# One encoder block on one core: keys and values of the first group computed token by token, V scaled by a column of 1/rms read back through DRAM

## The chip, the cores and the metric

The kernel runs on one NeuronCore of a Trainium2 chip. The metric is the device time of the core in microseconds; the median of the runs counts. One further execution was profiled, and all rows of the trace are from it.

## The reference

One block of an encoder for 256 tokens of width 2048, in float32. Shortened:

```python
u = rmsnorm(h, norm_mix_g)                       # D_MODEL 2048, SEQ 256
z = u @ w_in
b_a, c_a, v_a, q, k, v, gl_a, gl_b = split(z)    # 3 x 1024, q 1024, k 256, v 256, 2 x 2048
y_a = (b_a * centred_dwconv3(c_a * v_a, conv_a_w)) @ w_out_a
q, k = rope(q), rope(k)                          # 16 query heads, 4 key heads, 64 wide
att = banded_window_attention(q, k, v, sink)     # |distance| <= 128, a sink per head
y_b = att @ w_o_attn
h = h + (sigmoid(gl_a + b_a') * y_a + sigmoid(gl_b + b_b') * y_b) @ w_mix_out
up = centred_dwconv3(rmsnorm(h, norm_ffn_g) @ ffn_w_up, ffn_conv_w) + ffn_conv_b
h = h + (silu(up[:D_FF]) * up[D_FF:]) @ ffn_w_down
return rmsnorm(h, norm_final_g)
```

## The kernel before, in words

**Arithmetic.** Every float32 product is three products in TensorE's fp32r format. Weights and activations are split into a high part (a rounded copy) and a low part (what the rounding left), and hi x hi, hi x lo and lo x hi are added in one PSUM bank. ACT makes a weight chunk's high part (L203, tile `whi`), the DVE its low part (L214, tile `wlo`). The input x, transposed, stands in `xs` as 16 k-tiles of 128 rows with 256 columns hi and 256 columns lo; it is multiplied by the norm's weights there, while the division by the rms comes after the products.

**Two ways of a product.** A *single block* takes 128 output features: the weights are stationary, x is moving. L261 is a matmul of `whi` with 512 columns (x hi and lo), L262 one of `wlo` with 256 columns (x hi). The result has features on partitions and tokens along the row, as rotary embedding and scores need it. A *quad* takes 512 features at once: x is stationary, 128 tokens at a time, and the weights are moving, 512 columns. For each of the two halves of the tokens there are three matmuls, L237 (x hi, `whi`), L238 (x lo, `whi`) and L239 (x hi, `wlo`). Its result has tokens on partitions. To be turned, it goes through 32x32 transposes on the DVE (L330), a write to a DRAM tile `way` (L314) and four reads that put the blocks where they belong (L318, and L322 for a copy with the two halves of every head exchanged, which rotary embedding wants).

**The order of the work** is written out by hand. `run` goes through a list of chunks. Chunks 0 to 15 are the first group, one k-tile each: six single blocks K0, K1, V0, V1, Q0, Q1. Chunks 16 to 19 are the other two early query blocks (`w_q`, Q2 and Q3, eight k-tiles a chunk). Then come chunks of two k-tiles of a quad: 20 to 75 for seven quads of `w_in`, the first of them the last four query tiles (`rope_four`), the others the conv mixer; from 76 on the gates, then the output projections, the mixing matrix and the feed-forward part; at the end some single blocks again and the final norm. For each chunk c, `run` first issues the fetch of chunk c+6 (SyncE, L188), the cast of chunk c+3 (ACT) and the subtraction of chunk c+2 (DVE), and then chunk c's matmuls. `raw` has five buffers, `whi` four, `wlo` three, so these instructions wait for buffers that older chunks free.

Everything else is hung between chunks. A counter `now` goes up by one after each chunk's matmuls. An epilogue is a Python generator, and each `yield 1` in it means "go on after the next chunk". So "step n" below is what is issued after n chunks of matmuls, ahead of the fetch, cast and subtraction of that turn. All engines take their instructions in this written order, each in its own queue, and the waits for data are added by the framework. A tile with one buffer can be given out anew while its old contents have readers still to come in the written order: the first write of the new contents then waits for the last of them.

**What stands around the change.** `r1` (due at step 14) sums the squares of x, multiplies by a matrix of ones on TensorE (L390, step 16), and at step 18 has 1/rms in `r`, the same on all partitions, along the tokens; cos and sin are multiplied by it (L499). Singles are evacuated by `total` (L291 on ACT, L295 on the DVE), which adds the two halves of a bank. Keys and early queries then run through `rope`: four transfers on SyncE exchange the halves of a head (L535, tile `rot`), the DVE multiplies by cos and sin and adds (L537, L541, L542), `twice` copies the two heads of a tile to both halves of the partitions by four transfers (L550, tile `two`, one buffer), and ACT and the DVE make high and low parts: `kh` and `kl` for K (L557, L559), `qs` for queries (L566, L570). V is multiplied by `r`, turned on TensorE by four 128x128 transposes with an identity from the constants (`epi_v`, L619), and copied to `vtok` (L621), tokens on partitions.

`TURNS` (L127) has some single blocks issue lo before hi, at positions 1, 5, 9 and 15 from where `turns` was called: in the first group from chunk 4, and in the single blocks at the kernel's end.

Attention runs in ten blocks at steps 29 + 21t // 4. A block t issues the scores of two heads (L631, L632, eight matmuls), whose softmax runs on DVE and ACT and whose probabilities go through DRAM as above; from t = 3 on every second block also multiplies the probabilities by `vtok` (L684).

Of the kernel before, what the change touches and what calls it, by code (L numbers as in the profile page):

```python
# [45 lines left out]
C_ID = C_MASK + T  # L46
C_END = C_ID + P

# [5 lines left out]
def hybrid_block_kernel(  # L54
# [81 lines left out]
    taken = [0]  # L136

    def quad_banks():
# [3 lines left out]
        if q < IN_QUADS:  # L142

            where = l2 if q % 2 else [(lin, "ps"), (aps, "tp2")]
        else:
            where = ([(aps, "s0"), (aps, "s1")], [(aps, "tp2"), (aps, "av")], l2)[(q - IN_QUADS) % 3]
        return [pool.tile([P, QUAD * P], F32, tag=tag, name="pq") for pool, tag in where]

    def run(groups):
# [21 lines left out]

        def size(c):

            w, blocks, _ = chunks[c]
            return len(blocks) if w is None else w.shape[1]
# [41 lines left out]
        for c, (_, blocks, _) in enumerate(chunks):  # L217
# [7 lines left out]
            for i, (job, k) in enumerate(blocks):  # L225
                _, n, rhs, epi, *kind = job
                if kind == ["quad"]:
                    if k == 0:
# [4 lines left out]
                        w[:, QUAD * i : QUAD * i + QUAD, :].rearrange("p q f -> p (q f)") for w in (hi, lo)  # L233
# [9 lines left out]
                if was_quad[0]:  # L243
                    was_quad[0] = False
                    turns()
# [6 lines left out]
                if order["due"] and n >= KT:  # L252
# [8 lines left out]
                    lambda: nc.tensor.matmul(both, hi[:, i, :], moving, start=k == 0, stop=last and turned),  # L261
                    lambda: nc.tensor.matmul(  # L262
                        ps[:, 0:T], lo[:, i, :], a[:, 0:T], start=False, stop=last and not turned
# [169 lines left out]
    ident = ct[:, C_ID : C_ID + P]  # L433
# [54 lines left out]
    cs = {}  # L488

# [14 lines left out]
    def scaled(ps, dst=None):  # L504
        t = yield from total(ps)
        if dst is None:
            dst = spool.tile([P, T], F32, tag="evs", name="evs", bufs=4)
        nc.vector.tensor_tensor(dst, t, rr["r"], op=ALU.mult)
        return dst
# [20 lines left out]
    def rope(raw):  # L530
# [7 lines left out]
        yield 1  # L538
        yield 1
# [6 lines left out]
    def twice(rcos):  # L546
# [4 lines left out]
        yield 1  # L551
        yield 1
        return two

    def rope_k(raw):
        two = yield from rope(raw)
        nc.scalar.copy(kh, two)  # L557
        yield 1
        nc.vector.tensor_tensor(kl, two, kh, op=ALU.subtract)  # L559
# [12 lines left out]
    def epi_qk(i, ps):  # L572
# [4 lines left out]
        if i == 1:  # L577
            yield from rope_k(raw)
        elif i % 2 == 1:
            yield from rope_q(raw, i - 3)  # L580

    def rope_four(banks):
# [4 lines left out]
        f, rot = early_f  # L587
        yield from from_banks(banks, early_d)
        yield from by_dram(flat_f(f), flat_d(early_d), flat_f(rot), landing=1)
        for _ in range(3):  # L590
            yield 1
        for t in (4, 6):
            rcos = rope_buffers()[1]
            c, r = ([by_block_of_tokens(rcos[:, i, :]) for i in range(2)], [tile_of(rot, t - 4 + i) for i in range(2)])
            for i in range(2):
                nc.vector.tensor_tensor(c[i], tile_of(f, t - 4 + i), by_block_of_tokens(cs["cos"]), op=ALU.mult)
            yield 1
            for i in range(2):
                nc.vector.tensor_tensor(r[i], r[i], by_block_of_tokens(cs["sin"]), op=ALU.mult)
            yield 1  # L600
            for i in range(2):
                nc.vector.tensor_tensor(c[i], c[i], r[i], op=ALU.add)
            yield 1
            begin(lambda t=t, rcos=rcos: put_q(t, rcos))
        under_way[0] -= 2

# [3 lines left out]

    def epi_v(i, ps):
        v = p1.tile([P, T], F32, tag="vraw", name="vraw", bufs=2)
        yield from scaled(ps, v)

        for _ in range(3 + 3 * i):
            yield 1
        tp = aps.tile([P, 2, T], F32, tag="tp", name="vtp")
        for b in range(2):
            nc.tensor.transpose(tp[:, b, 0:P], v[:, b * P : (b + 1) * P], ident)  # L619
        yield 1  # L620
# [109 lines left out]
    def qk(i):  # L730
        return lambda ps: epi_qk(i, ps)
# [363 lines left out]
```

## Time and profile before

| | us |
|---|---|
| median of three runs | 1301.14 |
| lowest and highest | 1301.07, 1301.46 |
| the profiled execution | 1300.4 |
| its span, first to last instruction | 1298.6 |
| TensorE busy in the span | 1288.3 |
| DVE busy, ACT busy | 945.0, 660.3 |
| mean granted TensorE clock | 0.998 |

A row of the timeline has the start in us from the span's start, the duration in us, the engine, the line, the operation, the tiles (output <- inputs), the shape, how many neighbours were merged (x4), and in brackets how long the engine had been idle before and what ended that. `SPq` is a transfer's issue on SyncE, which isn't its landing. Matmuls overlap in the records (a 512-column matmul shows 0.39 us), so their pace is read from start to start. A row of the groups has the count behind x, then busy us and mean ns of one.

### The profile page before, as it was taken

How to read it: one execution, taken by the hardware profiler on the slowest of the kernel's cores; microseconds unless marked ns; L12 is line 12 of the kernel's file. 1: busy time of each engine (PE TensorE's matmuls, PEld its weight loads, DVE VectorE, ACT ScalarE, POOL GpSimd, SP SyncE). 2: the span in 40 equal slices, each digit the busy share in tenths (PEclk: the TensorE clock that was granted, in tenths of full speed). 3: DMA queues.
4: the chain of work that ended last, by engine and by line, in shares of the span. 5: the costliest groups of instructions: out<-in, count | busy, mean ns of one | idle time of the engine just before them, and what ended most of it. 6: DMA issues, size and time to landing. Idle time of an engine off the chain costs nothing.

```text
span 1298.6 us, 17037 instructions
## 1 busy us (share of the span) xinstructions
PE 1288.3 (99%) x5918; PEld 1071.8 (83%) x5918; DVE 945.0 (73%) x1404; ACT 660.3 (51%) x927; POOL 55.5 (4%) x67
## 2 busy tenths in 40 slices
PE   9999999999999999999999999999999999999997
PEld 8888888888888888888888888888888888888886
DVE  7888887665656686786788888787888885545454
ACT  7656665454444344445555545555555554434342
POOL 0000000000000000141000000000000000101031
PEclk9999999999999999999999999999999999999999
DMA  8799998878777887776777777767777676767662
GB/s 304 237 285 292 304 294 275 243 248 294 239 249 260 290 283 230 256 260 203 249 257 235 239 237 250 248 238 239 247 240 247 220 266 194 224 197 226 192 209 104
DMA packets 116310, 318.24 MB, mean 245 GB/s; under 512 B 13184, under 2 KB 45312, under 8 KB 116224
## 3 DMA queue, kind: packets, MB, share of 16 engines
q1 hardware_dynamic: 115648, 316.37, 74.5%
q8 instruction: 46, 0.75, 0.2%
q10 hardware_dynamic: 576, 0.79, 0.2%
q14 instruction: 40, 0.33, 0.1%
HBM read 280.15 MB, written 33.55 MB: 242 GB/s over the span
## 4 chain that ended last, share of the span: by engine, by line
PE 99%; DVE 0%; ACT 0%; issue 0%; POOL 0%; POOLq 0%; DVEq 0%; ACTq 0%
PE pq L237 30%; PE pq L239 30%; PE pq L238 30%; PE ps L261 5%; PE ps L262 3%; PE av L684 1%; PE warm L446 0%; PE s L631 0%; PE s L632 0%; PE more L910 0%; DVE y L952 0%; DVE x L917 0%; DVE r L944 0%; PE nps L390 0%; ACT ln L934 0%
## 5 line engine op out<-in xcount | busy, mean ns | idle before, releaser
L214 DVE TENSOR_TENSOR wlo<-raw,whi 128x1024 fp32r<-128x1024 f32 (+3 forms) x465 | 563.9, 1217 | 302.6 <-PE pq L239 156.2
L203 ACT CAST whi<-raw 128x1024 fp32r<-128x1024 f32 (+3 forms) x465 | 483.0, 1040 | 551.7 <-PE pq L238 382.5
L237 PE MATMUL pq<-whi,hs 128*128 128x512 f32 x704 | 274.0, 389 | 0.0
L239 PE MATMUL pq<-wlo,hs 128*128 128x512 f32 x704 | 273.9, 389 | 0.0
L238 PE MATMUL pq<-whi,hs 128*128 128x512 f32 x704 | 273.9, 389 | 0.0
L237 PE MATMUL pq<-whi,xs 128*128 128x512 f32 x480 | 187.1, 390 | 0.0
L239 PE MATMUL pq<-wlo,xs 128*128 128x512 f32 x480 | 186.9, 389 | 0.0
L238 PE MATMUL pq<-whi,xs 128*128 128x512 f32 x480 | 186.8, 389 | 0.0
L237 PEld LDWEIGHTS pq<-whi,hs 128*128 128x128 f32 x704 | 132.1, 188 | 27.5
L239 PEld LDWEIGHTS pq<-wlo,hs 128*128 128x128 f32 x704 | 132.1, 188 | 27.5
L238 PEld LDWEIGHTS pq<-whi,hs 128*128 128x128 f32 x704 | 132.1, 188 | 27.3
L239 PEld LDWEIGHTS pq<-wlo,xs 128*128 128x128 f32 x480 | 90.1, 188 | 18.9
L237 PEld LDWEIGHTS pq<-whi,xs 128*128 128x128 f32 x480 | 90.1, 188 | 18.7 <-issue 0.4
L238 PEld LDWEIGHTS pq<-whi,xs 128*128 128x128 f32 x480 | 90.1, 188 | 18.5
L330 DVE STREAM_TRANSPOSE qd<-pq 128x512 f32<-128x512 f32 x88 | 62.5, 710 | 5.8 <-PE pq L239 5.0
L237 PE MATMUL pq<-whi,actC 128*128 128x512 f32 x168 | 65.4, 389 | 0.0
L238 PE MATMUL pq<-whi,actC 128*128 128x512 f32 x168 | 65.4, 389 | 0.0
L239 PE MATMUL pq<-wlo,actC 128*128 128x512 f32 x168 | 65.4, 389 | 0.0
L412 ACT ACTIVATE up<-evs,vt 128x256 f32<-128x256 f32 x88 | 50.0, 592 | 0.0
L237 PE MATMUL pq<-whi,ya_att 128*128 128x512 f32 x128 | 49.8, 389 | 0.0
L238 PE MATMUL pq<-whi,ya_att 128*128 128x512 f32 x128 | 49.8, 389 | 0.0
L239 PE MATMUL pq<-wlo,ya_att 128*128 128x512 f32 x128 | 49.8, 389 | 0.0
(180 smaller groups left out, 1512.9 us busy)
## 6 DMA issues: line engine op xcount, KB each, us to landing
raw<-in_w_up_dram SPq DMA_DIRECT2D x176, 512.0 KB, 4.4
raw<-in_w_dn_dram SPq DMA_DIRECT2D x66, 512.0 KB, 4.0
raw<-in_w_gate_dram SPq DMA_DIRECT2D x64, 512.0 KB, 4.5
raw<-in_w_in_dram SPq DMA_DIRECT2D x56, 512.0 KB, 5.9
way<-qd SPq DMA_DIRECT2D x44, 512.0 KB, 2.9
qf<-way SPq DMA_DIRECT2D x176, 128.0 KB, 3.0
raw<-in_w_mix_dram SPq DMA_DIRECT2D x32, 512.0 KB, 4.3
raw<-in_w_end_dram SPq DMA_DIRECT2D x20, 512.0 KB, 4.0
```

The lines of the kernel that those rows point to most:

```text
L203: nc.scalar.copy(his[c][:, a:b, :], raws[c](a, b))
L214: nc.vector.tensor_tensor(los[c][:, a:b, :], raw(a, b), his[c][:, a:b, :], op=ALU.subtract)
L237: nc.tensor.matmul(ps, ah, wh, start=k == 0, stop=False)
L238: nc.tensor.matmul(ps, al, wh, start=False, stop=False)
L239: nc.tensor.matmul(ps, ah, wl, start=False, stop=last)
L261: lambda: nc.tensor.matmul(both, hi[:, i, :], moving, start=k == 0, stop=last and turned),
L262: lambda: nc.tensor.matmul(ps[:, 0:T], lo[:, i, :], a[:, 0:T], start=False, stop=last and not turned),
L330: nc.vector.transpose(d[:, :, h, :], ps)
L412: nc.scalar.activation(dst, src, AF.Identity, bias=bias, scale=w1)
L684: nc.tensor.matmul(o[64 * e : 64 * e + 64, i, :], vtok[:, b, v0 : v0 + HD], pT[:, e, b], start=b == 0, stop=b == 1)
```

## The change

1. K and V become one quad in the first group, Q0 and Q1 stay single blocks and come first. A chunk of the group is now Q0, Q1, then six quad matmuls. The quad's banks are `s0` and `s1`, those of Q0 and Q1 `tp2` and `av`.
2. K's turning, with its rotated copy, goes through DRAM as the last four query tiles' does (`turned_with_rows`, `rotated`), in place of `total` and `rope`.
3. V comes with tokens on partitions, so its four TensorE transposes, the identity and the epilogue are gone. It has to be multiplied by 1/rms along the partitions. For that `r1` writes one row of `r` to DRAM at step 18 and reads it back as a column `rcol` (128 partitions x 2) at step 20; ACT multiplies at step 23.
4. The waits in `rope` and `twice` are three steps in place of two; K's high part is made at step 28 (before 23), Q2's and Q3's epilogues start one step later, and attention blocks are at steps 32 + 21t // 4.
5. `turns` is due at step 16 in place of 4, so the turned blocks are among those of `w_q`.

```diff
     def quad_banks():
         q = taken[0]
         taken[0] += 1
-        if q < IN_QUADS:
+        if q < 0:
+            where = [(aps, "s0"), (aps, "s1")]
+        elif q < IN_QUADS:
...
-                if was_quad[0]:
+                if was_quad[0] and n > KT:
                     was_quad[0] = False
                     turns()
...
     def r1():
...
+        row = turn.tile([1, T], F32, tag="row", name="row")
+        nc.sync.dma_start(row, rr["r"][0:1, :])
+        yield 1
+        yield 1
+        nc.sync.dma_start(rcol, row.rearrange("o (h p) -> p (o h)", h=2))
...
     def rope(raw):
...
-        yield 1
-        yield 1
+        for _ in range(3):
+            yield 1
         for i in range(2):
             nc.vector.tensor_tensor(rot[:, i, :], rot[:, i, :], cs["sin"], op=ALU.mult)
...
     def twice(rcos):
         two = p1.tile([P, 2, 2, T], F32, tag="two", name="two")
...
-        yield 1
-        yield 1
+        for _ in range(3):
+            yield 1
         return two
...
+    def turned_with_rows(banks, waits):
+
+        f, rot = early_f
+        yield from from_banks(banks, early_d)
+        yield from by_dram(flat_f(f), flat_d(early_d), flat_f(rot), landing=1)
+        for _ in range(waits):
+            yield 1
+        return f, rot
+
+    def rotated(f, rot, m):
+        rcos = rope_buffers()[1]
+        c, r = ([by_block_of_tokens(rcos[:, i, :]) for i in range(2)], [tile_of(rot, m + i) for i in range(2)])
+        for i in range(2):
+            nc.vector.tensor_tensor(c[i], tile_of(f, m + i), by_block_of_tokens(cs["cos"]), op=ALU.mult)
+        yield 1
+        for i in range(2):
+            nc.vector.tensor_tensor(r[i], r[i], by_block_of_tokens(cs["sin"]), op=ALU.mult)
+        yield 1
+        for i in range(2):
+            nc.vector.tensor_tensor(c[i], c[i], r[i], op=ALU.add)
+        yield 1
+        return rcos
...
+    def keys_and_values(banks):
+
+        under_way[0] += 2
+        begin(lambda: values(banks))
+        f, rot = yield from turned_with_rows(banks, 3)
+        rcos = yield from rotated(f, rot, 0)
+        under_way[0] -= 2
+        two = yield from twice(rcos)
+        nc.scalar.copy(kh, two)
+        yield 1
+        nc.vector.tensor_tensor(kl, two, kh, op=ALU.subtract)
+
+    def values(banks):
+        for _ in range(7):
+            yield 1
+        for h, ps in enumerate(banks):
+            v = vtok[:, h, :].rearrange("p (i b j) -> p i b j", i=2, b=4)
+            nc.scalar.mul(v, ps.rearrange("p (b m j) -> p m b j", b=4, m=QUAD)[:, 2:4], rcol[:, h : h + 1])
...
-    def epi_v(i, ps):
-        v = p1.tile([P, T], F32, tag="vraw", name="vraw", bufs=2)
-        yield from scaled(ps, v)
...
-        for b in range(2):
-            nc.tensor.transpose(tp[:, b, 0:P], v[:, b * P : (b + 1) * P], ident)
-        yield 1
-        nc.scalar.copy(vtok[:, :, i * P : (i + 1) * P], tp[:, :, 0:P])
...
     first = [
         (None, KT, xr, qk(0)),
-        (None, KT, xr, qk(1)),
-        (None, KT, xr, after(1, lambda ps: epi_v(0, ps))),
-        (None, KT, xr, after(1, lambda ps: epi_v(1, ps))),
-        (None, KT, xr, after(2, qk(2))),
-        (None, KT, xr, after(3, qk(3))),
+        (None, KT, xr, after(1, qk(1))),
+        (None, KT, xr, keys_and_values, "quad"),
     ]
...
-    at(4, turns)
+    at(KT, turns)
...
-        groups.append(single(w_q[i], KT, xr, after(5 - i, qk(4 + i))))
+        groups.append(single(w_q[i], KT, xr, after(6 - i, qk(2 + i))))
...
-        at(29 + 21 * t // 4, block)
+        at(32 + 21 * t // 4, block)
```

Beside it, the weights are laid out in the new order, a chunk's blocks are counted by their width (a quad is four), and `rope_four` calls the two new helpers with what it did before.

More of the change, by code (lines that the diff above doesn't have):

```diff
@@ L134, in hybrid_block_kernel @@
     bank_tags = {}
-    taken = [0]
+    taken = [-1]
     def quad_banks():
@@ L170, in run, with width @@
         was_quad = [False]
+        def width(job):
+            return QUAD if job[4:] == ("quad",) else 1
         def size(c):
             w, blocks, _ = chunks[c]
-            return len(blocks) if w is None else w.shape[1]
+            return sum(width(job) for job, _ in blocks) if w is None else w.shape[1]
         def pieces(c):
@@ L224, in run @@
             ended = []
-            for i, (job, k) in enumerate(blocks):
+            i = 0
+            for job, k in blocks:
                 _, n, rhs, epi, *kind = job
+                w0, i = i, i + width(job)
                 if kind == ["quad"]:
@@ L260, in run @@
                 products = [
-                    lambda: nc.tensor.matmul(both, hi[:, i, :], moving, start=k == 0, stop=last and turned),
+                    lambda: nc.tensor.matmul(both, hi[:, w0, :], moving, start=k == 0, stop=last and turned),
                     lambda: nc.tensor.matmul(
-                        ps[:, 0:T], lo[:, i, :], a[:, 0:T], start=False, stop=last and not turned
+                        ps[:, 0:T], lo[:, w0, :], a[:, 0:T], start=False, stop=last and not turned
                     ),
@@ L488, in hybrid_block_kernel @@
     cs = {}
+    rcol = p1.tile([P, 2], F32, tag="rcol", name="rcol")
     def r1():
@@ L576, in epi_qk @@
         yield from total(ps, raw[:, i % 2, :])
[L577 to L580, printed above, removed]
+        if i % 2 == 1:
+            yield from rope_q(raw, i - 1)
+    def turned_with_rows(banks, waits):
[18 more added lines that the diff above has]
+        return rcos
     def rope_four(banks):
@@ L586, in rope_four @@
         under_way[0] += 2
[L587 to L591, printed above, removed]
-        for t in (4, 6):
[L593 to L603, printed above, removed]
+        f, rot = yield from turned_with_rows(banks, 3)
+        for t in (4, 6):
+            rcos = yield from rotated(f, rot, t - 4)
             begin(lambda t=t, rcos=rcos: put_q(t, rcos))
         under_way[0] -= 2
+    def keys_and_values(banks):
+        under_way[0] += 2
+        begin(lambda: values(banks))
+        f, rot = yield from turned_with_rows(banks, 3)
+        rcos = yield from rotated(f, rot, 0)
[10 more added lines that the diff above has]
+            nc.scalar.mul(v, ps.rearrange("p (b m j) -> p m b j", b=4, m=QUAD)[:, 2:4], rcol[:, h : h + 1])
     def put_q(t, rcos):
```

28 lines of the change are left out of this document (5 added, 23 removed).

## The prediction

> **What bounds the kernel now.** I read the page first, then the same execution cut into stages, then TensorE's timeline around the first two hundred microseconds, and last the two queues that feed it, the DVE and SyncE's.
>
> ```profile
> span 1298.6 us, 17037 instructions
> PE 1288.3 (99%) x5918; PEld 1071.8 (83%) x5918; DVE 945.0 (73%) x1404; ACT 660.3 (51%) x927; POOL 55.5 (4%) x67
> PE 99%; DVE 0%; ACT 0%; issue 0%; POOL 0%; POOLq 0%; DVEq 0%; ACTq 0%
> ```
>
> The chain that ended last is TensorE for 99%. A busy share alone doesn't show full pace, so I look at the stages that the change touches, and then at the spacing of the matmuls.
>
> ```profile
> 0.00:39.30 39.30, 37.85 (x203) 32.86 (x204) 29.84 (x48) 28.66 (x54) 0.20 (x4) 1.00 0.87 302
> 39.30:50.86 11.56, 11.56 (x68) 10.19 (x67) 9.63 (x21) 8.54 (x12) 0.00 (x0) 1.00 0.59 194
> 50.86:76.00 25.14, 25.14 (x115) 20.69 (x114) 20.05 (x30) 12.46 (x15) 0.00 (x0) 1.00 0.82 249
> 76.00:220.00 144.00, 144.00 (x694) 117.40 (x693) 123.88 (x236) 89.01 (x181) 0.00 (x0) 1.00 0.94 296
> ```
>
> These are the first group, the four chunks of w_q, the first projection quads, and the attention stage (columns: stretch, length, PE, PEld, DVE, ACT, POOL, granted clock, DMA share, GB/s). TensorE is never idle in them and its clock is 1.00. So the time can fall only by matmul work that goes away or runs closer together, and it can rise only where TensorE waits for data. Both are small things here, and I cost them one by one.
>
> ```profile
> 20.61 0.39 PE L261 MATMUL ps<-xs,whi 128*128 128x512 f32 x1
> 38.98 0.39 PE L261 MATMUL ps<-xs,whi 128*128 128x512 f32 x1
> L261 PE MATMUL ps<-xs,whi 128*128 128x512 f32 x53 | 18.4, 391 | 0.0
> 64.83 0.39 PE L239 MATMUL pq<-wlo,xs 128*128 128x512 f32 x1
> 75.70 0.39 PE L239 MATMUL pq<-wlo,xs 128*128 128x512 f32 x1
> L239 PE MATMUL pq<-wlo,xs 128*128 128x512 f32 x16 | 6.2, 389 | 0.0
> ```
>
> Between the first two rows lie 53 single blocks (a 512-column and a 256-column matmul each): 18.37 / 53 = 0.3466 us a block. Between the next two lie 16 rounds of three quad matmuls (L237, L238, L239): 10.87 / 48 = 0.2265 us each. Four single blocks cost 1.386 us a k-tile, a quad of six matmuls 1.359 us: 0.027 us less for the same columns, once the quad has settled.
>
> **The change part by part.**
>
> *V's transposes (out).* V was transposed on TensorE by four small matmuls, in two places.
>
> ```profile
> 53.63 0.38 PE L619 MATMUL vtp<-ct,vraw 128*128 128x128 f32 x2
> 53.76 0.48 PE L237 MATMUL pq<-whi,xs 128*128 128x512 f32 x1
> 62.20 0.48 PE L237 MATMUL pq<-whi,xs 128*128 128x512 f32 x1
> ```
>
> From 53.76 to 62.20 run three chunks, 36 quad matmuls, and the second pair of transposes: 8.44 us, of which 36 x 0.2265 = 8.15 are quads. One interruption, with the disturbed matmuls behind it, costs 0.29 us, two cost 0.57. They are gone: -0.57 us, straight off the chain.
>
> *K and V as a quad (four single blocks become one).* Each of the 16 chunks of the first group is now two single blocks, then six quad matmuls. At the settled paces this saves 16 x 0.027 = 0.43 us. But a switch of shape disturbs the pace:
>
> ```profile
> 76.88 0.40 PE L237 MATMUL pq<-whi,xs 128*128 128x512 f32 x1
> 78.27 0.39 PE L237 MATMUL pq<-whi,xs 128*128 128x512 f32 x1
> 14.27 0.39 PE L261 MATMUL ps<-xs,whi 128*128 128x512 f32 x1
> 20.26 0.40 PE L261 MATMUL ps<-xs,whi 128*128 128x512 f32 x1
> ```
>
> Behind the first score matmuls the six quads took 1.39 us, 0.2317 each. From 14.27 to 20.26 lie 17 single blocks among which four are turned (lo before hi): 0.3524 each. A chunk of the new kind switches twice in 2 us and may never settle: 2 x 0.3524 + 6 x 0.2317 = 2.095 us against 6 x 0.3466 = 2.080, that is +0.24 us over 16 chunks. So the bounds are -0.43 and +0.24. No row has such a mixed chunk; the nearest is the disturbed quad, so I take disturbed quads and settled singles, 2.083 us: +0.06. The turned blocks move from chunk 4 to the w_q chunks, where they cost the same 0.1 us: nothing.
>
> The Trainium skill would weigh this otherwise. "TensorE: Matmul & The Clock Gate", in its section on the back-to-back issue gap, gives a warm isolated matmul as its columns over 2.4 GHz plus 2.5 ns, so a quad (six matmuls) would beat four single blocks (eight) by two fixed costs, about 5 ns a k-tile or -0.08 us in all, an estimate from that page. The trace disagrees on the size: 226.5 ns where the formula has 215.8. By the page the sum below would be 0.14 us lower.
>
> *V's other work.* Its evacuations and multiplications on ACT and DVE go, two ACT multiplications by the column of 1/rms come at step 23, and the 128 columns of identity are no longer loaded. (Step n: what is issued after n chunks of matmuls.) All of this lies beside TensorE, which is a chunk or more behind those engines. At one place it was tight:
>
> ```profile
> 49.13 1.22 DVE L214 TENSOR_TENSOR wlo<-raw,whi 128x1024 fp32r<-128x1024 f32 x1
> 50.86 0.39 PE L237 MATMUL pq<-whi,xs 128*128 128x512 f32 x1
> ```
>
> Chunk 20's low half ended at 50.35, half a microsecond before its matmuls, because step 18 put K's and V's vector work behind r. Now it holds less, so no wait appears there.
>
> *K's transfers and the column of 1/rms.* K's quad brings SyncE one `way` write and eight reads for four rotary transfers, at steps 17 to 19.
>
> ```profile
> 46.01 0.52 SPq L188 DMA_DIRECT2D raw<-in_w_in_dram  x1
> 53.60 1.05 ACT L203 CAST whi<-raw 128x1024 fp32r<-128x1024 f32 x1 [1.60 <-PE pq L238]
> 81.88 1.75 SPq L318 DMA_DIRECT2D early<-way  x4
> ```
>
> Five transfers more are about 2.2 us at L318's 0.44 each, and SyncE also stands until the write has landed. Chunk 24's fetch (46.01) would go some 3 us later and land some 53 us in, when its cast (53.60) begins anyway; its matmuls come at 62.20. So this costs nothing; were it 3 us more, the cast would still be 4 us early. The row of 1/rms leaves on SyncE at step 18, behind the wait for r, and is read back at step 20. Queued behind them are K's transfers and the fetches of chunks 24 and 26. ACT needs the column at step 23.
>
> ```profile
> 59.21 1.06 ACT L557 CAST kh<-two 128x1024 fp32r<-128x1024 f32 x1 [1.56 <-DMA two<-rcos]
> DMA to landing us min/median/max: 2.2/3.9/6.4
> DMA to landing us min/median/max: 3.5/5.6/8.7
> ```
>
> The first row is step 23 on ACT, 59.2 us. The others are the landing times of the `two` transfers (40 to 130 us) and of the w_in fetches (35 to 130 us). I expect the read to be issued near 54 us, since the eight rotary transfers of step 19 precede it. Bounds 2.2 and 8.7: it lands between 56 and 63; I take 4 us, by the small `two` transfers. Even at 63 it costs TensorE nothing, since a cast is done over 7 us ahead of its use (chunk 24: 54.65 against 62.20). In a sentence by itself: "DMA: Bandwidth & Descriptors", in its rules for kernel authors, says that a strided last dimension becomes one descriptor per element, and the specifications there name 512 bytes as the least for full rate, so these 256 elements of 4 bytes are the slow kind; no row here has one, and the rival it makes is below.
>
> *Rotary transfers get three chunks; blocks come at 32.* This removes ACT's waits for `two` and DVE's for `rot`, none of which reached TensorE: nothing gained. The last block moves to step 79, and what it writes is read by the attention output projection more than 64 chunks later: nothing lost.
>
> *A new hold on SyncE.* Tile `two` has one buffer. Q0/Q1 fill it at step 23 and are finished with it at step 27 (L570's two subtractions). K, now from the quad, wants it at step 25. So SyncE stands from step 25 until step 27, with the fetches of chunks 31, 32 and 33 behind it. The kernel before has such a hold, within step 40:
>
> ```profile
> 108.97 1.41 DVE L570 TENSOR_TENSOR qs<-two,qs 64x512 fp32r<-64x512 f32 x2
> 110.44 2.39 SPq L550 DMA_DIRECT2D two<-rcos  x4
> 114.94 0.44 SPq L188 DMA_DIRECT2D raw<-in_w_in_dram  x1
> DMA to landing us min/median/max: 5.3/5.3/5.3
> ```
>
> The transfers start when the subtractions end (110.38), the next fetch follows them and lands 5.3 us later. For the new place:
>
> ```profile
> 67.28 0.81 SPq L188 DMA_DIRECT2D raw<-in_w_in_dram  x2
> DMA to landing us min/median/max: 3.5/4.3/5.1
> 69.80 1.41 DVE L570 TENSOR_TENSOR qs<-two,qs 64x512 fp32r<-64x512 f32 x2 [0.55 <-ACT qs L566]
> 73.18 1.06 ACT L203 CAST whi<-raw 128x1024 fp32r<-128x1024 f32 x1 [1.27 <-PE pq L238]
> 78.86 1.22 DVE L214 TENSOR_TENSOR wlo<-raw,whi 128x1024 fp32r<-128x1024 f32 x1
> 82.35 0.39 PE L237 MATMUL pq<-whi,xs 128*128 128x512 f32 x1
> 75.93 0.28 PE L631 MATMUL s<-kh,qs 128*128 128x256 f32 x1
> ```
>
> The subtractions of step 27 ended at 71.21; half a microsecond earlier now, 70.6. Four transfers of `two` take 2.4 us: 73.0. Chunk 31's fetch then starts, in place of 67.7. It lands after 3.5 to 8.7 us; I take 3.5 to 5.3, by the two fetches that also followed a hold: 76.5 to 78.3. Cast 1.06, subtraction 1.22 and two hand-overs of 0.1: ready at 79.0 to 80.8. Before it, the DVE takes K's subtraction (1.2) and a transpose (0.7), behind K's landing at 75 to 77 and its cast: about the same moment. TensorE used chunk 31 at 82.35. It now comes there 0.57 earlier, and another 0.95 earlier since the score block of step 29 (75.93 to 76.88) comes only at 32: 80.8, and it needs the low half 0.45 later, 81.3. So the data are 0.5 to 2.3 us early: no wait, but a thin cover. If it goes (a landing of 5.8 us or more), each microsecond over is one on the chain. Chunk 32 has the 0.95 of that score block more.
>
> **The sum.** -0.57 + 0.06 = -0.5 us. The profiled execution took 1300.4 us, 1.8 outside its span of 1298.6; it would take 1299.9. The median of the runs before is 1301.14, 0.7 above it, and 1301.14 - 0.5 = 1300.6; a tenth or two for short waits behind the hold makes 1300.8 us, which I forecast. A measurement of this kernel can tell about 0.2%, 2.6 us, so that is no change.
>
> **The rivals.**
> *The quad runs at its settled pace inside the mixed chunk.* For it: single blocks settle within two blocks after another shape. Against: quads took six or more. Then 1301.14 - 0.57 - 0.43 = 1300.1 us.
> *The gain is given back behind the hold.* A landing near 7 us leaves TensorE waiting 1.2 us at chunk 31, and the late DVE hands a part on: 1301.0 to 1303.5. For it: DMA share 0.82 there, the stage's longest landing 8.7. Against: while SyncE stands, nothing else is in flight.
> *Slower: the same hold, long.* A landing of 8.7 us is 2.9 over the cover: 1300.6 + 2.9 = 1303.5; with another 0.3 on chunk 32 or 33 it passes 1303.74. It decides from a landing of 9 us on, or if SyncE is freed 3 us later than I worked out.
> *The column is late.* Were the read of 256 elements to take over 12 us (5 to ACT's step 23 and 7 of cover), TensorE would wait for the cast behind it; at 14 us, 2 us: 1302.6. No row is near this.
> *The change does nothing:* the transposes' 0.57 us is eaten by mixed chunks at their upper bound (+0.24) and by w_q's 32 single blocks, if all run at 0.3524 (+0.19): 1301.0.
>
> **How the numbers follow.** Forecast 0.52, settled quad 0.12, nothing 0.08, given back 0.19, late column 0.01: all within 0.2%, 0.92. The long hold 0.07, slower. Faster by over 0.2% would need 2.6 us out of a stream whose removable work is 1.0 us: 0.01. The range runs from the settled quad less half the spread of the runs (1300.1 - 0.2 = 1299.9) into the given-back case, 1303.0, which leaves out some 0.1 above.
>
> **What would show it.** Right: no L619 rows; TensorE without idle time from 6 us on; the 16 mixed chunks 33.2 to 33.5 us long; the second set of `two` transfers starting just as the first L570 pair ends; chunk 31's fetch issued 4 to 6 us later than in the kernel before and landing before 79. Wrong: a gap in the quad matmuls near 80 us, or fetches behind the row of 1/rms issued so late that a gap shows at chunks 24 to 26; and, for the gain, quads at 0.2265 in the mixed chunks.

## The result, and the profile after

The kernel after takes 1309.26 us (median of six runs, 1307.16 to 1310.38), the kernel before 1301.12 beside it (six runs, 1300.87 to 1301.46). The ratio is 1.0061, with an interval of 1.0048 to 1.0074: slower by 8 us. The forecast was 1300.8, with nothing over 1303.0 in its range.

First the same parts of the page as before: the totals, and the chain of waits. The profiled execution took 1310.4 us.

```profile
span 1308.6 us, 16969 instructions
PE 1292.2 (99%) x5882; PEld 1071.6 (82%) x5882; DVE 945.0 (72%) x1401; ACT 659.9 (50%) x923; POOL 55.5 (4%) x67
PE 94%; DMA 3%; DVE 2%; SPq 0%; issue 0%; ACT 0%; POOL 0%; POOLq 0%; DVEq 0%; ACTq 0%
```

TensorE still has 99% of the span, and that tells nothing; the chain does. It was TensorE for 99%, now DMA and DVE have 5% of it. The stages show where (columns as before; the last row is a part of the one above it):

```profile
0.00:39.30 39.30, 37.85 (x172) 31.35 (x173) 30.84 (x49) 28.42 (x54) 0.20 (x4) 1.00 0.85 301
50.86:76.00 25.14, 25.14 (x113) 20.78 (x112) 17.91 (x26) 11.64 (x14) 0.00 (x0) 1.00 0.82 238
76.00:220.00 144.00, 138.39 (x642) 111.30 (x641) 118.58 (x231) 86.70 (x177) 0.00 (x0) 0.98 0.92 279
135.41:141.40 5.99, 5.99 (x22) 4.42 (x23) 2.75 (x6) 3.56 (x8) 0.00 (x0) 0.50 1.00 400
```

The first group is as it was. The loss lies in the attention stage, 76 to 220 us: TensorE is busy for 138.4 of 144 us, and for six more it ran at a granted clock of 0.50. What TensorE waited for between 30 and 240 us (us in total, times, longest):

```profile
PE av L697 <- DMA pT<-way: 4.5, 1, 4.5
PE pq L245 <- DVE wlo L218: 0.5, 1, 0.5
PE pq L243 <- ACT whi L207: 0.4, 1, 0.4
```

The long wait is at the first product of probabilities and V (step 47), for the last read of the turned probabilities. TensorE's timeline there, with a matmul of the usual pace at the end:

```profile
135.41 1.97 PE L697 MATMUL av<-pT,vtok 128*64 128x256 f32 x8 [4.48 <-DMA pT<-way]
139.62 0.63 PE L244 MATMUL pq<-whi,xs 128*128 128x512 f32 x1
140.04 0.63 PE L245 MATMUL pq<-wlo,xs 128*128 128x512 f32 x1
142.33 0.39 PE L243 MATMUL pq<-whi,xs 128*128 128x512 f32 x1
142.56 0.40 PE L244 MATMUL pq<-whi,xs 128*128 128x512 f32 x1
```

A 512-column matmul took 0.42 us from start to start behind the wait, 0.23 before and later. So one wait costs twice: 4.5 us of standing, and 3.0 us (half of 6.0) of half pace. With the two short waits of 0.9 us, that is 8.4 of the 9.5 us by which this span stands above that of the same kernel without any wait (1299.1, below). Around the short waits the matmuls are also slower (0.34 us from start to start right behind them, in place of 0.23), which would account for part of the rest; I have not split it further.

The chain says what was late (start, length, what; a fetch or a write counts until it has landed):

```profile
70.01 0.35 DVE qs L569
70.42 0.47 SPq L555
...
72.86 3.82 DMA raw<-in_w_in_dram
76.79 0.72 DVE early L336
77.66 8.10 DMA way<-early
85.77 0.33 SPq L324
...
87.62 5.58 DMA raw<-in_w_in_dram
93.21 0.30 SPq L328
93.61 4.77 DMA raw<-in_w_in_dram
98.47 1.06 ACT whi L207
...
122.21 8.17 DMA raw<-in_w_in_dram
130.40 4.74 DMA pT<-way
135.41 1.97 PE av L697 x8
```

It begins where the prediction looked, at the hold on `two`: the subtraction of Q1 ends, K's transfers go at 70.42, chunk 31's fetch at 72.86. That fetch landed at 76.68, in time. What came behind it did not: a turning write took 8.1 us to land, chunk 36 was fetched at 87.62 and chunk 37 at 93.61, and TensorE waited at 99. At 130.40 the read of the probabilities went right behind the landing of an older fetch (122.21 + 8.17 = 130.38). That looks like a limit of the queue: counted from issue to landing, SyncE never has more than eight transfers under way in the kernel before, where all 820 landings are on record, and this read was again the eighth, as far as the landings around it are on record.

Two more views, side by side. What SyncE waited for between 60 and 125 us in the kernel after, two of the rows; and its DMA share in two stretches of 4 us.

```profile
SPq L555 <- DVE qs L569: 9.5, 2, 6.9
SPq L555 <- DMA two<-rcos: 5.2, 1, 5.2
68.00:72.00 4.00, 4.00 (x19) 3.34 (x18) 3.58 (x6) 2.96 (x3) 0.00 (x0) 1.00 0.29 98
116.00:120.00 4.00, 4.00 (x20) 3.24 (x19) 3.90 (x9) 2.06 (x3) 0.00 (x0) 1.00 0.45 103
```

There are two holds on `two`, not one: K behind Q0 and Q1 (until 70.4) and the last query pair behind the second last (steps 40 and 41, until 116.9). The first row has 2.6 us of the first hold and all 6.9 of the second; the second row is the rest of the first hold, in which K's copies wait until those of Q0 and Q1 have landed. From 62.5 to 70.4 us SyncE issues nothing. In both holds the DMA engines run empty (0.29 and 0.45 busy in these stretches, 0.00 from 70 to 71 and from 116 to 117 us), while over 76 to 220 us they are 0.92 busy. The kernel before has a hold at step 40 too (4.1 us, DMA share 0.71 from 108 to 112 us), and TensorE doesn't wait there: a hold costs nothing as long as the data keep some time to spare.

### The profile page after: what moved, and what is told of

It reads as the page before. It is cut to its first block, busy times and chain, and to the rows that moved or that the text cites. A ratio compares the mean times of both kernels' runs of the same rounds, so it can differ in the third digit from the quotient of the medians.

```text
span 1308.6 us, 16969 instructions
## 1 busy us (share of the span) xinstructions
PE 1292.2 (99%) x5882; PEld 1071.6 (82%) x5882; DVE 945.0 (72%) x1401; ACT 659.9 (50%) x923; POOL 55.5 (4%) x67
## 4 chain that ended last, share of the span: by engine, by line
PE 94%; DMA 3%; DVE 2%; SPq 0%; issue 0%; ACT 0%; POOL 0%; POOLq 0%; DVEq 0%; ACTq 0%
PE pq L243 29%; PE pq L245 29%; PE pq L244 29%; PE ps L267 4%; DMA raw<-in_w_in_dram 2%; PE ps L268 2%; DMA way<-early 1%; PE av L697 1%; DVE wlo L218 1%; DMA pT<-way 0%; PE warm L451 0%; PE s L644 0%; DVE st L656 0%; PE s L645 0%; SPq L555 0%
## 5 line engine op out<-in xcount | busy, mean ns | idle before, releaser
L245 PE MATMUL pq<-wlo,xs 128*128 128x512 f32 x512 | 200.3, 391 | 0.8 <-DVE wlo L218 0.5
L243 PE MATMUL pq<-whi,xs 128*128 128x512 f32 x512 | 200.2, 391 | 0.4 <-ACT whi L207 0.4
L244 PE MATMUL pq<-whi,xs 128*128 128x512 f32 x512 | 200.0, 391 | 0.0
L245 PEld LDWEIGHTS pq<-wlo,xs 128*128 128x128 f32 x512 | 96.4, 188 | 22.8 <-DVE wlo L218 2.5
L243 PEld LDWEIGHTS pq<-whi,xs 128*128 128x128 f32 x512 | 96.5, 189 | 20.7 <-ACT whi L207 0.6
L244 PEld LDWEIGHTS pq<-whi,xs 128*128 128x128 f32 x512 | 96.4, 188 | 19.4
L336 DVE STREAM_TRANSPOSE qd<-pq 128x512 f32<-128x512 f32 x88 | 62.5, 710 | 5.9 <-PE pq L245 5.0
```

The costliest lines, as they stand in the source:

```text
L243: nc.tensor.matmul(ps, ah, wh, start=k == 0, stop=False)
L244: nc.tensor.matmul(ps, al, wh, start=False, stop=False)
L245: nc.tensor.matmul(ps, ah, wl, start=False, stop=last)
L336: nc.vector.transpose(d[:, :, h, :], ps)
```

## The experiments

**The theory.** Each hold takes transfer time away. The stage needs nearly all the transfer time there is, so it isn't made up, and all that SyncE carries from there on is late, until TensorE waits where the data have the least time to spare. **Rivals:** (B) the third wait and the later blocks cost it, whatever K's copy does; (C) the hold costs by SyncE standing, so another queue would do; (D) the engines are crowded, and only fewer or earlier transfers help; (E) the half pace after a wait is the cost, and one wait in one place makes it.

All medians are in us; the kernel before is the one timed beside each.

| run | median (lowest to highest, runs) | before | ratio (interval) |
|---|---|---|---|
| e1, K's copy in a buffer of its own | 1304.34 (1301.78–1308.34, 10) | 1301.0 | 1.0026 (1.0016–1.0036) |
| e2, query copies with two waits | 1305.76 (1304.9–1308.79, 4) | 1301.0 | 1.0047 (1.003–1.0063) |
| e3, before, blocks at 32 | 1301.0 (1300.2–1301.77, 10) | 1301.0 | 1.0001 (0.9992–1.001) |
| e4, e1 and e2 | 1300.56 (1300.2–1303.11, 10) | 1301.0 | 1.0001 (0.9992–1.001) |
| e5, copies from GpSimd's queue | 1309.99 (1307.37–1311.58, 4) | 1300.56 | 1.0069 (1.0052–1.0086) |
| e6, before, blocks at 32 and three waits | 1304.8 (1304.03–1306.68, 5) | 1300.56 | 1.0033 (1.002–1.0046) |
| e7, TensorE kept busy at step 47 | 1308.87 (1308.01–1309.5, 4) | 1300.56 | 1.0063 (1.0048–1.0078) |
| e8, own buffers for K and the last pair | 1301.02 (1300.52–1304.24, 10) | 1300.56 | 1.0007 (0.9998–1.0016) |
| e9, K's copy two steps later, two waits | 1304.01 (1302.47–1304.9, 10) | 1300.85 | 1.002 (1.0011–1.0029) |
| e10, before, three waits | 1301.65 (1300.76–1304.24, 10) | 1300.85 | 1.0006 (0.9997–1.0015) |
| e11, first product with V two steps later | 1306.94 (1305.15–1308.38, 4) | 1300.85 | 1.0042 (1.0028–1.0055) |
| e12, e8 and e11 | 1301.07 (1300.11–1302.64, 11) | 1300.85 | 0.9999 (0.999–1.0008) |
| e13, probabilities on GpSimd's queue | 1308.33 (1306.52–1308.58, 4) | 1300.61 | 1.0052 (1.0037–1.0067) |
| e14, e9 and e13 | 1309.17 (1307.36–1310.26, 4) | 1300.61 | 1.0058 (1.0041–1.0076) |
| e15, half fetches, chunks 33–40 | 1304.53 (1301.34–1306.85, 10) | 1300.75 | 1.0025 (1.0016–1.0035) |
| e16, half fetches, chunks 52–59 | 1307.89 (1306.05–1309.44, 4) | 1300.75 | 1.0057 (1.004–1.0074) |
| e17, half fetches, chunks 33–48 | 1301.0 (1300.43–1302.77, 10) | 1300.9 | 1.0001 (0.9992–1.001) |
| e18, own buffer for the last pair alone | 1303.42 (1302.4–1308.58, 10) | 1300.9 | 1.0027 (1.0015–1.0038) |

### Which part costs it: e1 to e4, e6, e10

e1, e2 and e4 are the kernel after with the helper below and its first call (K's copy in the tile `pd` of the probabilities, which isn't in use yet), its second call, and both:

```diff
-    def twice(rcos):
-        two = p1.tile([P, 2, 2, T], F32, tag="two", name="two")
+    def twice(rcos, tag="two", waits=3):
+        two = p1.tile([P, 2, 2, T], F32, tag=tag, name="two")
...
-        two = yield from twice(rcos)              # K
+        two = yield from twice(rcos, "pd")
...
-        two = yield from twice(rcos)              # put_q
+        two = yield from twice(rcos, waits=2)
```

> The changed kernel, but K's copy to both halves of the partitions gets a buffer of its own (the tile of the probabilities, free until block 0), so SyncE no longer stands from step 25 to 27. Theory H (this hold crowds the fetches and starts the waits): chunks 31 to 33 are fetched before 69 us in place of 72.9 to 76.5, TensorE's waits at chunks 36 to 46 (2 to 3 us together) go, and most of the 4.9 us at the first probabilities-times-V too: 1300.5 to 1303. Rival C (the shift of the attention blocks by three chunks makes block 1 share its steps with the second quad's turning): the early waits go, the long one stays with its slow clock: 1305 to 1308. Rival P (the third wait in the copy lengthens the hold at step 40): as C, 1305 to 1308.

> The changed kernel, but the last four query tiles wait two steps behind their copies, as before, not three; so the hold at step 40 ends a step earlier. K's hold stays. Theory H: within 1.5 us of the changed kernel, 1307.5 to 1310. Rival P: the long wait at the first probabilities-times-V goes, 1302 to 1304. Rival C: 1307 to 1310.

> The changed kernel with both edits: K's own buffer, and two waits for the last four query tiles. Theory H: as with K's own buffer alone, 1300.3 to 1302. Rival P: 1300.3 to 1302 here, but not with K's own buffer alone. Rival C: 1304 to 1308, the long wait still there.

e3 is the kernel before with `at(32 + 21 * t // 4, block)` in place of 29.

> The kernel before with one edit: attention blocks at steps 32 + 21t // 4 in place of 29. Theory H and rival P: no change, 1300.5 to 1302, since there is no hold at step 25 and the step-40 hold is the short one. Rival C: block 1's write and reads meet the second quad's at steps 41 and 43, TensorE waits some 3 to 5 us at step 47 and runs at half clock behind it: 1304 to 1309.

Of the 8.1 us, e1 leaves 3.3 over its kernel before, e2 4.8, and both edits together none that the runs can tell. e1 and e2 each lie between the times that their expectations gave. Neither K's copy nor the third wait is the whole cause. In e1 the short waits are gone and one of 2.5 us is left at the first product with V; in e2 it is the other way round:

```profile
PE av L697 <- DMA pT<-way: 2.5, 1, 2.5
```
```profile
PE pq L245 <- DVE wlo L218: 1.1, 2, 0.5
PE pq L243 <- ACT whi L207: 0.5, 2, 0.3
PE av L697 <- DMA pT<-way: 0.2, 1, 0.2
```

So the two edits mend two different places. e3 shows that the later blocks alone cost nothing that can be measured. What the third wait does, with and without them, is asked in the kernel before, where K isn't in `two` at all:

```diff
-    def twice(rcos):
+    def twice(rcos, waits=2):
...
-        two = yield from twice(rcos)              # put_q
+        two = yield from twice(rcos, 3)
...
-        at(29 + 21 * t // 4, block)
+        at(32 + 21 * t // 4, block)               # e6 only
```

> The kernel before with two edits of the change: attention blocks at 32 + 21t // 4, and three waits in place of two behind the last four query tiles' copies. No quad for K and V. Theory: the hold at step 40 lasts into step 41 and costs by itself, as it did with K's own buffer: a wait of 2 to 3 us at the first probabilities-times-V, 1303.5 to 1305. Rival (it costs only on top of what K's quad has delayed): 1300.5 to 1302.

> The kernel before with one edit: three waits in place of two behind the last four query tiles' copies; blocks stay at 29. Theory T (the longer hold at step 40 costs alone): 1303 to 1305.5. Rival M (it costs because the blocks at 32 put the first block's reads behind it; with blocks at 29 there is more room): 1300.3 to 1301.7.

Blocks at 32 cost 0.0, the third wait 0.8 (an interval that reaches below nothing), both together 4.2 us. The third wait makes the second hold longer by a step; blocks at 32 bring the second block's probabilities to SyncE just behind that hold (the copies go at 112.38, at 110.44 in the kernel before). Either alone stays under the cover, together they don't. That settles rival B: it is a part of the cause, and not without the hold (e8, below, has the third wait and the later blocks but no hold).

### The two holds, one by one: e8, e18

```diff
-    def twice(rcos):
-        two = p1.tile([P, 2, 2, T], F32, tag="two", name="two")
+    def twice(rcos, two=None):
+        if two is None:
+            two = p1.tile([P, 2, 2, T], F32, tag="two", name="two")
...
-        two = yield from twice(rcos)              # K; e8 only
+        two = yield from twice(rcos, p1.tile([P, 2, 2, T], F32, tag="pd", name="two"))
...
+        own = box["B"][:, 14:16, :].bitcast(F32).rearrange("p e (i t) -> p e i t", i=2) if t == 6 else None
-        two = yield from twice(rcos)              # put_q
+        two = yield from twice(rcos, own)
```

> The changed kernel with all its three-step waits, but K's copy and the last query pair's copy each have a buffer of their own (the probabilities' tile, and the part of the attention output's tile that is written last). Neither hold is left. Theory H+P (holds cost, waits don't): 1300.0 to 1301.2, no wait of TensorE over 0.5 us. Rival (the third wait costs by lateness, not by the hold): 1303 to 1305, as with K's own buffer alone.

> The kernel after, with a buffer of its own for the copy of the last query pair alone, so that the second hold is gone; K's copy stays in the one-buffer tile, so that the first hold stays. It completes the four cases with K's own buffer alone (1304.3), both (1301.0) and neither (1309.3). Theory (each hold takes transfer time that isn't made up, and they add up): the waits at chunks 36 to 46 stay, with 1 to 2.5 us together; the reads of the first probabilities come earlier, and TensorE's wait there is shorter than 4.9 us: 1302.5 to 1306. Rival (the first hold costs nothing that lasts once the second is gone): under 1302. Other rival (the first hold alone costs it all): 1307 or more.

e8 keeps the three waits, the blocks at 32, K and V as a quad and the column through DRAM; only the holds go. TensorE has no wait left between 76 and 220 us, and the stretches in which the DMA engines ran empty are full:

```profile
68.00:72.00 4.00, 4.00 (x19) 3.32 (x18) 3.94 (x6) 2.37 (x3) 0.00 (x0) 1.00 1.06 266
76.00:220.00 144.00, 144.00 (x687) 118.05 (x686) 123.45 (x238) 89.17 (x180) 0.00 (x0) 1.00 0.94 292
116.00:120.00 4.00, 4.00 (x19) 3.31 (x18) 3.87 (x7) 3.09 (x7) 0.00 (x0) 1.00 1.03 420
```

The four cases, each over its kernel before: both holds 8.1 us, the first taken away (e1) 3.3, the second taken away (e18) 2.5, neither left (e8) 0.5. Each hold alone costs some 3 us, both 8, more than the sum: with both, the second hold ends later (the last copies go at 116.86, at 113.74 in e1). e18's profile has the short waits alone, and no half pace (its clock is 1.00 from 76 to 220 us), as the theory had it:

```profile
PE pq L243 <- ACT whi L207: 1.0, 1, 1.0
PE pq L245 <- DVE wlo L218: 0.5, 1, 0.5
```

This is the test that carries the explanation.

### Is it the queue, or what the engines carry: e5, e13, e14, e15 to e17

e5 has `nc.gpsimd.dma_start` for the copies to `two`, so that SyncE doesn't stand. e13 gives the write and the reads of the probabilities to GpSimd's queue (`queue=nc.gpsimd` through `by_dram`), e14 does so in e9.

> The changed kernel with one edit: the copies to both halves of the partitions (tile two, all four sets) are issued by GpSimd's queue, not by SyncE's. Buffer, steps and the wait for the buffer stay, so K's copies start no earlier; only what stands behind them in a queue changes. Theory H (SyncE standing at the copies is what costs): fetches of chunks 31 to 33 go out before 70 us, no wait of TensorE over 1 us, 1300.2 to 1302. Rival D (the transfers themselves crowd the DMA engines, whoever issues them): 1305 to 1310 as the changed kernel.

> The changed kernel with one edit: the probabilities' way through DRAM (one write and four reads a block) is issued by GpSimd's queue, not by SyncE's. Both holds stay. Theory Q (SyncE's queue, in its written order and with eight transfers in flight at most, is what makes the first probabilities late): the reads of block 1 go out some 3 us earlier, the long wait and the slow matmuls behind it go, the waits at chunks 36 to 46 stay: 1302 to 1305. Rival D (the DMA engines are crowded, whichever queue issues): the reads land no earlier, 1307 to 1310.

> The kernel with K's copies at step 27 and two waits for the last query tiles (1304.0), with the probabilities' transfers on GpSimd's queue. It had no waits of TensorE but the one at the first probabilities-times-V. Theory Q: that one goes, 1300.3 to 1301.7. Rival D: 1303 to 1305 as before.

None gained beyond the spread of the runs. In e5 SyncE did go on through the hold, but K's copies, issued from 71.70, landed only at 80.34, ACT's cast of them stood in its queue with the casts of the next chunks behind it, and TensorE waited there instead:

```profile
PE pq L243 <- ACT whi L207: 2.2, 2, 1.4
PE pq L245 <- DVE wlo L218: 2.0, 2, 1.3
```

In e13 the reads went out at 123.5 to 125.2, 3.7 to 5.2 us earlier than in the kernel after, and the last of them landed at 133.8, 1.4 us earlier, after 7 to 9 us. The wait at the first product fell from 4.5 to 0.8 us there and no half pace followed, but 4.2 us of other waits stand in its profile. So the order of issue (rival C) isn't all that holds the reads; how much is under way seems to be. "DMA: Bandwidth & Descriptors" of the Trainium skill says in its section on issuing engines that transfers from any engine run on the same sixteen DMA engines, and another issuer saves only the time to issue. These runs agree: 1309.99, 1308.33 and 1309.17 us against 1309.26. e14 is 5 us slower than e9, which neither branch of its expectation had; why stays open.

The direct test takes load off the DMA engines and leaves every queue as it is. Part of the computation is left out: the second half of some weight chunks is a constant.

```diff
-                nc.sync.dma_start(raw[:, : w.shape[1], :], w)
+                if 33 <= c < 41:                  # e16: 52 to 59; e17: 33 to 48
+                    half = w.shape[1] // 2
+                    nc.gpsimd.memset(raw[:, half : w.shape[1], :], 0.01)
+                    nc.sync.dma_start(raw[:, :half, :], w[:, :half, :])
+                else:
+                    nc.sync.dma_start(raw[:, : w.shape[1], :], w)
```

> This is the kernel after, but of the fetches of chunks 33 to 40 only the first half of each weight chunk is read from DRAM (0.25 MB of 0.5); the other half is set to a constant by GpSimd, which is otherwise idle there. So 2 MB of transfers are left out between about 73 and 110 us, some 7 us of the DMA engines at the 284 GB/s that they moved there; part of the weights is left out of the computation with it. Number, order and queue of the transfers are unchanged, and SyncE stands for the two holds as before. Theory (the DMA engines idle while SyncE stands, are full from 76 us on and so cannot make it up): with 7 us of room against some 3 us lost, the fetches and the reads of the first probabilities land in time, TensorE's wait at the first product of probabilities and V is under 1 us, no half pace: 1300.5 to 1303. Rival (the order of SyncE's queue and the waits on it set the lateness, whatever the engines carry): the reads are issued as late as before, 1306 to 1310.

> The same edit, at chunks 52 to 59, whose fetches come behind the first product of probabilities and V. It leaves out the same 2 MB and the same part of the weights, but after the waits. Theory: room that comes after the waits does not help, 1306.5 to 1310, with the wait at the first product of probabilities and V as in the kernel after (2 to 5 us) and half pace behind it. If the constant weights or the work on GpSimd themselves changed the time, it would show here: a time below 1305 would put the other run's gain in doubt.

> The edit of the half fetches at chunks 33 to 48 in place of 33 to 40: 4 MB left out (and the same half of those weights out of the computation), now also around the second hold, in which SyncE stood from 108 to 114 us and the DMA engines fell to 0.32 (112 to 116 us) with half fetches at 33 to 40 alone. Theory (transfer time lost in both holds, not made up while the DMA engines are full): the first product of probabilities and V waits under 1 us, no half pace, 1300.8 to 1303. Rival (after the second hold the reads of the probabilities are late by the order of the queue, whatever the engines carry): again a wait of 2 us or more there and half pace behind it, 1303.5 to 1306.

e15 came out between theory and rival: 1304.5. Its profile, of the slowest of its ten runs, has none of the waits at chunks 36 to 46, though chunk 31's fetch was as late as in the kernel after (74.36), but a wait of 3.4 us at the first product with V. Its second hold had emptied the engines again:

```profile
112.00:116.00 4.00, 4.00 (x23) 3.46 (x22) 3.94 (x8) 3.49 (x5) 0.00 (x0) 1.00 0.32 103
PE av L702 <- DMA pT<-way: 3.4, 1, 3.4
```

My expectation named both holds, but the room it made lies ahead of the second. e17 relieves both and is back at 1301.0, with both holds in place:

```profile
112.00:116.00 4.00, 4.00 (x23) 3.46 (x22) 3.94 (x7) 4.00 (x6) 0.53 (x1) 1.00 0.00 0
```

In its profile, again of the slowest run, a wait of 1.7 us is left, where I had expected less than 1. e16, the same 2 MB as in e15 left out behind the waits, stays at 1307.9; its profile has a wait of 3.1 us, but not the half pace that I had expected behind it. So idle time of the DMA engines costs nothing in itself; it costs because of the load behind it. Rival D, which is the theory's second half, is shown with one reservation: half fetches also land sooner and free SyncE's places sooner, and these runs don't separate that from the load on the engines.

### Other ways out, which failed: e7, e9, e11, e12

e7 puts 18 matmuls whose result is not used (4.1 us) ahead of the first product with V, so that TensorE doesn't idle there. e9 gives K's rotary two more steps of waiting, so that it comes behind Q0 and Q1 by itself, and takes put_q back to two waits. e11 has the first product with V two steps later, e12 the same in e8.

> The changed kernel with 18 more matmuls of 512 columns (4.1 us) on a spare bank ahead of the first probabilities-times-V, where TensorE waited 4.5 us and then ran some 5 us at 0.427 us a matmul. Their result isn't used. If the slow matmuls come from the wait, they go: 1309.3 less 2 to 3 us, 1306 to 1307.5. If they come from anything else, or if the wait is set by data that come no sooner and the slow part by the load: 1309 to 1313.

> The changed kernel with K's rotary steps two chunks later, so that its copies are written behind the subtractions that free the one buffer, and two waits for the last query tiles. K's data come no earlier than in the changed kernel. Theory (what costs is a transfer that stands in a queue ahead of work that could go on; late data alone do not): as with own buffers, 1300.2 to 1302. Rival (K's copies come too late, wherever they are written): 1304.5 to 1307, as with the two waits alone.

> The changed kernel with one edit: the first two probabilities-times-V come two steps (5.4 us) later, at step 49. Both holds stay. If the wait of 4.5 us there and the slow matmuls behind it are as large as the profile shows, they go and the waits at chunks 36 to 46 stay: 1309.3 less 5 to 7 us, 1302 to 1304.5. If the lateness is handed on to the next chunks and blocks: 1305 to 1309.

> The changed kernel with own buffers for both copies and the first probabilities-times-V two steps later. Theory: with own buffers alone the probabilities landed only 0.5 us ahead of their use, which made single runs of 1304; with two steps more all runs lie within 1 us: median 1300.2 to 1300.7, 0.3 to 0.8 us under the kernel before. Rival (the spread has another cause): median near 1301 and single runs of 1303 or more.

e7 missed its 1306 to 1307.5. In its profile the half pace is gone and the wait is 0.2 us, and its span is 1306.2; but that was the fastest of its four runs, and the median is only 0.4 lower than after's. The 4.1 us of added matmuls stand where the wait stood. The half pace is a part of the cost, but rival E, one wait in one place as the whole of it, falls: the profiles of e11 and e13 have no half pace either, and their medians are 1306.9 and 1308.3. e9 missed too. Its short waits are gone, as in e1, yet the first product with V waited 2.3 us, with half pace behind. The DMA engines had less idle time around the hold than in the kernel after (share 0.71 at the lowest, from 72 to 76 us), and it still cost 3.2 us. What exactly makes its reads late stays open, and with it how much of the cost the holds explain where K's data come late. e11 missed its 1302 to 1304.5 and came out in its other branch: with the product later, the lateness went to other places, 4.3 us in six waits of up to 1.6. e12 missed its 1300.2 to 1300.7: it and e8 can't be told apart.

## Why the prediction was wrong, point by point

**The sum of matmul work: right.** No matmuls with an identity are left. The first group took 33.63 us before and 33.64 after, where +0.06 for mixed chunks and -0.1 for turned blocks were forecast; a mixed chunk takes 2.087 us (forecast 2.083). From the first norm's matmul, behind the first group, to the second norm's, at about 601 us, e8 takes 561.04 us and the kernel before 561.43: 0.4 less, where -0.57 and +0.1 were forecast. None of it shows in a measurement: e4, e8 and e12 stand at 1.0001, 1.0007 and 0.9999.

**The column of 1/rms: right.** It was read at 55.69 and landed 4.3 us later, within the 56 to 63 that I gave; ACT's multiplications began at 60.34. e8 keeps it and has no wait.

**"A new hold on SyncE": right where it looked, and it looked at one chunk.** Transfers at 70.42 (forecast 70.6), fetch at 72.86 (73.0), landed 76.68 (76.5 to 78.3), low half ready 79.09 (79.0 to 80.8), used 81.14 (81.3): early by 2.05 us. The gap that it named as a sign of being wrong, near 80 us, didn't come; the gaps came at 99 us and from 131 us on. The step that failed is the sentence "So the data are 0.5 to 2.3 us early: no wait, but a thin cover", taken as the whole price of the hold: the sum has "a tenth or two for short waits behind the hold", and the measured price of the holds is some 8 us (1309.26 with both, 1301.02 without). Chunk 31 is only the first thing behind the hold. The low half of chunk 36 was ready 0.12 us ahead of its use (95.61 and 95.73), and TensorE waited for chunk 37. The hold took the DMA engines' time away (0.29 busy for 4 us, 1.06 without it), and the prediction quotes the row that should have raised the question whether that can be made up: DMA share 0.94 from 76 to 220 us. The share alone doesn't answer it (the kernel before has its own dips, 0.58 from 64 to 68 us, and no wait); e15 to e17 do. I used the share of the stage ahead of it (0.82) in a rival, as a risk to one landing, and not this one. "While SyncE stands, nothing else is in flight" was counted as a reason for a short landing; it was the loss itself.

**"Rotary transfers get three chunks; blocks come at 32": wrong.** "Nothing gained", "nothing lost" holds for either alone (e3 0.0, e10 0.8) and not for both (e6, 4.2 us). The working named the hold within step 40 and quoted its rows, as a model for the new one; that the third wait makes that hold itself longer was not followed up. And I costed the last block at step 79, not the first product with V, where the longest wait came.

**The price of a wait: missing.** Each microsecond over the cover was to be one on the chain, and the time was to rise "only where TensorE waits for data". A wait of 4.5 us cost 7.5, because of the half pace behind it.

**The rivals.** "Slower: the same hold, long" has the right place and sign. Its mechanism is not what happened: it needed a landing of 9 us at chunk 31, which was 3.8. "The gain is given back behind the hold" is nearest in words ("the late DVE hands a part on") and short by 6 us.

No version here beats the kernel before by what can be measured. K and V as a quad, with the column and blocks at 32, cost nothing that the runs can tell once both copies have a buffer (e8), or K's copy has one and the query copies wait two steps (e4).

## What to carry to other kernels

When a change makes a queue stand, don't stop at the first transfer behind it: look at the share of the DMA engines in the stage that follows, and where it is as high as here (0.92 to 0.94), count the time in which they run empty as lost for everything up to the point with the least time to spare, until a run shows otherwise. Look for all places where the same one-buffer tile is waited for; two edits that are free alone can meet in one of them. Here a buffer mended it, and another queue did not.

## What the runs showed of the hardware

Whether half pace follows a wait isn't decided by the wait's length alone. Three profiles, e6, e17 and e16, at the same eight matmuls:

```profile
130.96 1.51 PE L684 MATMUL av<-pT,vtok 128*64 128x256 f32 x8 [1.95 <-DMA pT<-way]
```
```profile
130.78 1.08 PE L702 MATMUL av<-pT,vtok 128*64 128x256 f32 x8 [1.66 <-DMA pT<-way]
```
```profile
134.79 1.08 PE L702 MATMUL av<-pT,vtok 128*64 128x256 f32 x8 [3.10 <-DMA pT<-way]
```

After 1.95 us of idle time the matmuls slowed down (granted clock 0.50 from 133 to 134 us); after 1.66 us they didn't (1.00), and after 3.10 us they didn't either (1.00 from 134.79 to 141.40 us). The traces' clock records show what differs. The clock changes in whole steps of 3.41 us, counted from its rise at the start of the run: in e6 it is full for 126.29 us (37 steps) and half for one step, in the kernel after full for 129.71 (38 steps) and half for two. e6's idle time lies within one step. That of e16 is split, 1.39 and 1.71 us in two steps. Over all the profiles, up to 1285 us, every one of the eight drops came behind a step with 1.95 us of idle time or more, and no step at full clock with 1.71 or less was followed by one. So where a wait falls among the steps matters, and the steps begin at a different time in each execution (4.3 to 7.7 us). The Trainium skill, in "TensorE: Matmul & The Clock Gate", the table on why this matters, advises against idle gaps of over some 3 us, by a window of activity that runs on its own (its Part 1). The steps agree with such a window; 1.95 us within one was enough here, and 3.10 us over two was not. Short waits, as in e2 (up to 0.5 us each), didn't slow it.

The time from issue to landing depends on what is under way: in e15 the copies to `two` landed in 2.2 us right behind the first hold (71.92 to 74.14) and in 8.3 us ahead of it (60.24 to 68.51).
